# S5 mixer with FFN on one core: modulation products, lag buffers and the order behind the scan

## The chip, the core and the metric

The kernel runs on one core of a Trainium2 chip. A core has five engines that run their own instruction streams: PE (TensorE, matrix products), DVE (VectorE), ACT (ScalarE), POOL (GpSimd) and SP (SyncE), which here only issues DMAs. DMAs are also issued from ACT and POOL. The metric is device time in microseconds (us), the median over runs. A profiled execution gives the trace from which everything below is read.

## The reference

One layer of a diffusion backbone: 1024 latent tokens and 256 context tokens of width 1024. The layer's mixer is a bidirectional S5 state-space model with 64 groups of 16 channels and 64 complex states for each group; a SwiGLU feed-forward follows. Only the latent stream is returned. Everything is float32.

```python
m_l = jnp.split(sc @ ada_w[i] + ada_b[i], N_MOD, axis=-1)       # sc = silu(c), six vectors of 1024
h_l = modulate(rms_norm(x, norm_mix[i]), m_l[0][:, None], m_l[1][:, None])
...
lam_bar = jnp.exp(lam * jnp.exp(log_step.astype(F32))[:, None])
b_bar = ((lam_bar - 1.0) / lam)[..., None] * lax.complex(b_re.astype(F32), b_im.astype(F32))
...
bu = jnp.einsum('lgh,gnh->lgn', u.astype(F32), b_bar)
_, h = lax.associative_scan(_linear_combine, (a, bu), axis=0)
return jnp.einsum('lgn,ghn->lgh', h, c_mat).real, h[-1]
...
g = jax.nn.gelu(y)
return g * jax.nn.sigmoid(g @ w_glu + b_glu)
...
x = x + m_l[2][:, None] * y_l
h_l = modulate(rms_norm(x, norm_ffn[i]), m_l[3][:, None], m_l[4][:, None])
x = x + m_l[5][:, None] * swiglu(h_l, ffn_w1[i], ffn_w3[i], ffn_w2[i])
```

## The kernel before

The order of every engine is the order in which the program is written (a manual schedule); waits come from the data and from the buffers.

The 1280 tokens are cut into chunks of 8 tokens: 32 context chunks and 128 latent chunks. The kernel computes, for each chunk, the state that its 8 tokens add ("sums"); scans these chunk states over the chunks; and then forms the output of a chunk from two parts: the state before the chunk times output weights, and the chunk's own 8 tokens times a table of the products at all 15 lags from -7 to 7 ("lags"). Indices: `hb = 2b + d` is a head, eight groups (b) and a direction (d); `q` is a quarter, 16 groups; a unit `u` has four groups, and `k` is a pair of units.

**Sums** (L558 to L593). For each of the 16 heads PE multiplies the chunks by input weights (L473), ACT copies the result into the states `ST` (L477 to L480), and DVE or POOL adds neighbouring states (`pair`, `ctx_low`). Input weights come from products on DVE or POOL (`bl_make`), an accumulating DMA of POOL (`bl_sum`, L333) and transposes on PE (`bl_tr`, L346). The loop also loads tiles of the modulation weights (`ada_load`, L417) and multiplies them (`ada`, L424): one tile is 128 x 512, and one product is one matrix product of a tile with silu(c). There are 64 such tiles. The first 16 products are done before the sums. `ada_load(m)` issues loads up to tile m; `ada(n)` does the products up to n and keeps eight loads ahead. In the loop, head 9 loads four tiles, head 11 multiplies them and loads four more, and head 14 multiplies these and loads six.

**Scan** (`scan`, L651). DVE alone: 95 dependent steps of four operations (`step`), and in the gaps of the first ones the operations that fill in the states of quarters 0 and 2 (`fill_ops`), two for each step. The fills of quarter 0 are complete after step 36.

**Behind the scan's start**, the string given to `run` (L806) is the order of the other engines' work, while DVE scans. Its letters:

- `An`: modulation products up to n. `M0` to `M2`: their result is copied, transposed and made into columns; M1 ends on ACT, M2 is on POOL.
- `Cqp`: output weights of quarter q, part p (`cl_gen`): two products on POOL, the first into `CL[q]`, the second into a buffer of `cts`, and their sum, which `HOW` puts on PE (L546, two times eight groups, with a copy on ACT, L547) or on an accumulating DMA that POOL issues (`SY`, L549).
- `Ki`: lag products of half a quarter (`k_mats`): for each of two group sets PE's products into `kt`, a copy on ACT into a buffer of `KX`, and a DMA from there to DRAM (`kd`, L633), also issued by ACT.
- `Tu`: the table of unit u, read back from DRAM by a DMA of SP (`toeplitz`, L641, four buffers `KQ`).
- `Rk`: ACT's copies of the states of the first 64 chunks for pair k (L729). `Pk`: PE's inner products of the pair: chunk times table (L747), states times weights (L752). `Yu`: ACT's copy of the result (L803). `Zi`: the same states for the last 64 chunks.
- `Fqh`: POOL's fills of quarters 1 and 3. `Li`, `Gi`: load and sign of `Cs`, from which C is made. `Bi`: ACT's copies of input weights that later K steps read.

Behind the string come the products of the last 64 chunks (`late_mm`, L827), GELU and GLU, and the feed-forward, which fills PE.

Each DMA of SP and ACT takes the next of eight semaphores in the order of the program and waits until the previous DMA on the same one has landed.

Of the kernel before, what the change touches and what calls it, by code (L numbers as in the profile page):

```python
# [17 lines left out]
P = 128  # L18
# [5 lines left out]
T = 8  # L24
G = 64
HC = 16
# [11 lines left out]
def s5_ffn_kernel(tc, a, out):  # L38
    nc = tc.nc
    V, S, E, PE, SY = nc.vector, nc.scalar, nc.gpsimd, nc.tensor, nc.sync  # L40
    ctx = ExitStack()
    with ctx:
# [5 lines left out]
        def view(reg, kb, shape, parts=P):  # L48
            off = int(round(kb * 256))
            n = int(np.prod(shape))  # L50
            v = reg[:parts, off:off + n]
            if len(shape) > 1:
                names = "abcdef"[:len(shape)]
                v = v.rearrange(f"p ({' '.join(names)}) -> p {' '.join(names)}",
                                **{k: d for k, d in zip(names, shape)})
            return v

        R0 = region("r0", 7)
        RA = region("ra", 80.5)
        RU = region("ru", 40)  # L60
        RC = [region(f"c{i}", 16) for i in range(4)]
        RXa, RXc = region("rxa", 8), region("rxc", 8)
# [22 lines left out]
        def small(shape, parts=P):  # L85
            v = view(R0, pos[0], shape, parts)
            pos[0] += int(np.prod(shape)) / 256
            assert pos[0] <= 7, pos[0]
            return v

        cpk = small([HC + 3 * P + HC + 4 + T + 16 + 16])
# [7 lines left out]
        S5 = int(round(pos[0] * 256))  # L99
        cols = small([2, 2, G])  # L100
        LS = small([2, 3, G])
        KD = small([4, 4, HC])
        scs, sc3 = small([8, 2]), small([8, 3])
        rsb, mod2, epsc = small([P + 32]), small([2, T]), small([2])
        mcol = small([4, T])
        ssq, ss2, rt, rtt = small([T, 4]), small([T]), small([T]), small([T])
        frs = small([T])
# [171 lines left out]
        LH = view(RXc, 0, [2, 3, G])  # L279
        SQ = [LS[:, 0], view(RXc, 2, [3, G]), LH[:, 0], LH[:, 1], LS[:, 1]]  # L280

# [122 lines left out]
        NA = 16  # L404
        stg = [view(RA, i, [512]) for i in (20, 22, 0, 2, 4, 6, 8, 10, 40, 42, 44, 46, 12, 14, 16, 18)] + [view(RC[2], 8 * (1 - i // 4) + 2 * (i % 4), [512]) for i in range(8)]
        ada_at = [0, 0]

        def ada_tile(i):

            return stg[i if i < NA else NA + (i - NA) % 4 if i < NA + 8 else NA + (i - NA) % 8]  # L410

        def ada_load(m):
            while ada_at[0] < min(64, m):
                i = ada_at[0]
                h, k, b = i // 32, i // 4 % 8, i % 4
                c0 = (2 + b) * D + 512 * h
                SY.dma_start(ada_tile(i), adaw[k * P:(k + 1) * P, c0:c0 + 512])  # L417
                ada_at[0] += 1

        def ada(n, top=64):  # L420
            for i in range(ada_at[1], n):
                ada_load(min(i + 8, top))
                h, k, b = i // 32, i // 4 % 8, i % 4
                PE.matmul(pm[32 * b:32 * b + 2], sc3[:, k, 1 - h:3 - h], ada_tile(i), start=i < 4, stop=i >= 60,  # L424
                          tile_position=(0, 32 * b))
                ada_at[1] += 1
# [129 lines left out]
        ct0 = [view(RC[1], i, [8, T, HC]) for i in (12, 4)]  # L556
        ct1 = [view(RC[3], i, [8, T, HC]) for i in (0, 4)]
        for hb in range(16):  # L558
            sums(hb)
            if hb == 0:  # L560
                bl_make(6)
                bl_sum(5)
            if hb % 2:
                for i in range(hb + 2, min(hb + 4, 16)):
                    bl_tr(i)
            bl_sum(hb + 6)
            if hb == 1:
                SY.dma_start(BXY[:, 1], a["bxy"][:, 3])
            bl_make(hb + 7)
            if hb < 6:  # L570
                u_ctx(hb + 2)
                u_lat(hb + 2)
                rs_lat(hb + 5)
            if hb >= 1:
                pair(hb - 1, E if hb - 1 in PPAIR else V)
            if hb == 9:
                cs_load(0)
            if hb == 12:
                cs_sign(0)
            if hb == 9:  # L580
                ada_load(NA + 4)
            if hb == 11:
                ada(NA + 4, NA + 4)
                ada_load(NA + 8)
            if hb == 14:
                ada(NA + 8, NA + 8)
                ada_load(NA + 14)
            if hb == 15:
                ada_load(NA + 16)
            if hb in CLOW:  # L590
                ctx_low(*CLOW[hb])
            for part in CGEN.get(hb, ()):
                cl_gen(0, part, ct0[part % 2], E if part == 3 else SY)  # L593
# [10 lines left out]
        kt = pA.tile([P, 2, 240], F32, tag="r3", name="kt")  # L604
        S.copy(kt.rearrange("p a b -> p (a b)"), cpk[:, 0:1].to_broadcast([P, 480]))


        KX = [cpk[:, HC + P:HC + P + 15 * HC], cols.rearrange("p a b g -> p (a b g)")[:, 0:15 * HC]]
        BBc = PW.rearrange("p t i (d e) -> p (t i) d e", d=2)
        KQ = [view(RA, 2 * i, [4, P]) for i in range(4)]  # L610
        HSe = [(RA, 8 + 4 * i) for i in range(2)]
        KD_ = [dr.tile([P, 4, 15 * HC], F32, tag=f"kd{q}", name=f"kd{q}") for q in range(4)]
# [4 lines left out]
        def k_mats(q, hq):  # L617

            for g_ in range(2):
                gq = 2 * hq + g_  # L620
                quarters = [(gi * 4 + gq, kt[32 * gi:32 * gi + HC, g_], (0, 32 * gi)) for gi in range(4)]
                for gl, kv, tp in quarters:
                    PE.matmul(kv[:, 128:240], bb(q, 1, gl), CL[q][:, 1, gl, 7:0:-1], start=True, stop=True, tile_position=tp)
                for gl, kv, tp in quarters:
                    PE.matmul(kv[:, 0:112], bb(q, 0, gl), CL[q][:, 0, gl, 6::-1], start=True, stop=True, tile_position=tp)
                for gl, kv, tp in quarters:
                    l0 = tp[1]
                    PE.matmul(kv[:, 112:128], ident[:, l0:l0 + HC], KD[:, q, gq], start=True, stop=False, tile_position=tp)
                for d in range(2):
                    for gl, kv, tp in quarters:  # L630
                        PE.matmul(kv[:, 112:128], bb(q, d, gl), Cs[q % 2][:, 0, d, gl], start=False, stop=d == 1, tile_position=tp)
                S.copy(KX[g_], kt[:, g_])
                S.dma_start(KD_[q][:, gq], KX[g_])  # L633

        def toeplitz(u):

# [117 lines left out]

        scan()
        inner, hse = {}, {}
        ct2 = [view(RC[3], i, [8, T, HC]) for i in (8, 12)]
        ct3 = [view(RXc, 4, [8, T, HC]), view(RU, 16, [8, T, HC])]
        cts = [ct0 * 2, ct1 * 2, ct1 * 2, ct2 + ct3]

        HSl = [hstate(RXc, 0), hstate(RXc, 4), hstate(RA, 8), hstate(RA, 0)]
        order = (6, 7, 4, 5, 0, 1, 2, 3)
# [6 lines left out]
        def run(prog):  # L769


            for w in prog.split():
                op, i = w[0], int(w[1:])
                if op == "A":
                    ada(i)
                elif op == "M":
                    mod_cols(i)
                elif op == "K":
                    k_mats(*divmod(i, 2))
                elif op == "Z":  # L780
                    late_restack(i)
                elif op == "L":
                    cs_load(i, S)
                elif op == "G":
                    cs_sign(i)
                elif op == "B":
                    j = 48 - HC * i
                    S.copy(BBc[:, :, :, j:j + HC], BB[:, :, HC * i:HC * i + HC].rearrange("p d g h -> p g d h"))
                elif op == "C":
                    q, part = divmod(i, 10)  # L790
                    cl_gen(q, part, cts[q][part], HOW[q][part])
                elif op == "F":
                    fill(*divmod(i, 10), *((RA, 12) if i < 20 else (RXc, 4)))
                elif op == "T":
                    toeplitz(i)
                elif op == "R":
                    hse[i] = hstate(*HSe[len(hse) % 2])
                    for d in range(2):
                        restack(hse[i], 4 * i, d, 0, 64, (S, S, S, S))
                elif op == "P":  # L800
                    inner_mm(i, hse[i])
                elif op == "Y":
                    S.copy(yview(i), inner[i])  # L803

        HOW = ((PE,) * 4,) + ((SY,) * 4,) * 2 + ((SY, SY, SY, PE),)
        run("A36 C00 A40 C01 A44 C02 A48 C03 A52 A56 K0 A60 K1 A64 L2 C10 T0 T1 T2 T3 C11 M0 M1 C12 C13 F10 F11 G2 B3 B2 K2 K3 L3"  # L806
            " R0 P0 C20 T4 T5 R1 P1 Y0 Y1 C21 M2 T6 T7 G3 C22 C23 R2 Y2 Y3 P2 R3 Y4 Y5 P3 Y6 Y7 K4 K5 T8 T9 T10 T11"
            " C30 C31 C32 R4 P4 R5 C33 K6 K7 Y8 Y9 P5 Y10 Y11 T12 T13 T14 T15 F30 F31 R6 P6 R7 Y12 Y13 P7 Z1 Z0 Y14 Y15")
        psA.__exit__(None, None, None)


# [289 lines left out]
        G2 = region("c1", 16, R32)  # L1101
# [307 lines left out]
```

## Time and profile before

| | us |
|---|---|
| median of 3 runs | 1119.66 (1116.76 to 1124.03) |
| profiled execution, its own time | 1125.31 |
| profiled execution, its span | 1123.5 |
| PE busy | 997.6 |
| DVE busy | 821.6 |
| POOL busy | 646.7 |
| ACT busy | 414.9 |

The span goes from the first to the last instruction. A row of a timeline reads: start, duration, engine, line, operation, what it writes and reads, how many instructions were merged, and in brackets the idle time before it and what ended that. "128x512 f32" are partitions and elements. SPq and ACTq are DMA issues of SP and ACT. A float32 matrix product counts as two passes, so that x8 at L424 is four products. An `r` in a name is the tile `R0`, `c` one of the four tiles `RC`, `ra`, `ru`, `rxa` and `rxc` the other regions. Some names of releasers are of an engine that had long been done: the wait of R0 at 206.35 is put down to DVE, while ACT was issuing a load.

### The profile page before, as it was taken

What the parts mean: (1) busy time and instruction counts of PE and PEld (TensorE: products, weight loads), DVE (VectorE), ACT (ScalarE), POOL (GpSimd) and SP (SyncE); (2) the same over time, 40 slices, a digit from 0 to 9 for tenths busy, and PEclk for the clock granted to TensorE, in tenths of its full rate; (3) what the DMA queues carried; (4) which work ended last, traced back from release to release, by engine and by line L of the source; (5) the groups of instructions that cost most, each with busy time, mean ns of one, the idle gap of its engine ahead of it and who ended that gap; (6) DMA issues with size and microseconds to landing.
All of it is one profiled execution on the core that took longest, in us unless ns stands there. A gap on an engine that the chain in (4) does not pass through costs nothing. (4 is left out here: it accounts for less than half of the span.)

```text
span 1123.5 us, 16549 instructions
## 1 busy us (share of the span) xinstructions
PE 997.6 (89%) x6088; PEld 802.1 (71%) x6088; DVE 821.6 (73%) x1689; ACT 414.9 (37%) x871; POOL 646.7 (58%) x503
## 2 busy tenths in 40 slices
PE   4689795647979999879999999999999999999997
PEld 1268422535869997667888888888888888888875
DVE  8989699980777796998666766666666666666657
ACT  4279512634834455222222222222222222222236
POOL 4389678882373343865555555555555555555563
PEclk9699897768999999899999999999999999999999
DMA  9966679753411201101111111111111111111104
GB/s 351 339 139 122 166 255 238 162 113 73 159 50 65 76 1 57 56 20 57 57 57 43 37 36 54 57 57 57 57 57 57 57 57 57 57 57 57 49 27 150
DMA packets 51457, 103.64 MB, mean 92 GB/s; under 512 B 4272, under 2 KB 25008, under 8 KB 49328
## 3 DMA queue, kind: packets, MB, share of 16 engines
q1 hardware_dynamic: 43456, 85.67, 23.0%
q0 software_dynamic: 3600, 13.11, 6.3%
q10 hardware_dynamic: 4320, 3.81, 1.0%
q8 instruction: 48, 0.79, 0.3%
q14 instruction: 33, 0.27, 0.1%
HBM read 83.30 MB, written 6.16 MB: 80 GB/s over the span
## 5 line engine op out<-in xcount | busy, mean ns | idle before, releaser
L70 POOL TENSOR_TENSOR c<-rxc,c 128x512 fp32r<-128x512 f32 x128 | 169.3, 1337 | 186.9 <-ACT c L1063 182.9
L70 DVE TENSOR_TENSOR ru<-pd,ru 128x512 f32<-128x512 f32 x336 | 227.0, 691 | 2.4 <-PE pd L1119 2.3
L1119 PE MATMUL pu<-ra,c 128*128 128x512 f32 x432 | 168.5, 390 | 1.3 <-POOL c L70 1.2
L1118 PE MATMUL pu<-ra,c 128*128 128x512 f32 x432 | 168.2, 389 | 0.6 <-DVE ra L70 0.6
L1117 PE MATMUL pu<-ra,c 128*128 128x512 f32 x432 | 168.4, 390 | 0.3 <-ACT ra L1063 0.3
L1063 ACT CAST c<-rxc 128x512 fp32r<-128x512 f32 x128 | 76.7, 616 | 186.2 <-POOL rxc L70 107.2
L1117 PE MATMUL pd<-c 128*128 128x512 f32 x336 | 133.2, 397 | 10.9 <-DVE ru L70 10.9
L1118 PE MATMUL pd<-c 128*128 128x512 f32 x336 | 132.4, 394 | 0.0
L1119 PE MATMUL pd<-c 128*128 128x512 f32 x336 | 132.2, 393 | 0.0
L70 DVE TENSOR_TENSOR ru<-pu,ru 128x512 f32<-128x512 f32 x84 | 57.9, 690 | 87.5 <-PE pu L1119 53.3
L70 POOL TENSOR_TENSOR c<-ru,c 128x1024 fp32r<-128x1024 f32 x22 | 53.2, 2420 | 85.8 <-ACT c L861 77.1
L1119 PEld LDWEIGHTS pu<-ra,c 128*128 128x128 f32 x432 | 81.1, 188 | 19.7 <-POOL c L70 3.0
L1118 PEld LDWEIGHTS pu<-ra,c 128*128 128x128 f32 x432 | 81.1, 188 | 17.7 <-POOL c L70 0.9
L1117 PEld LDWEIGHTS pu<-ra,c 128*128 128x128 f32 x432 | 81.1, 188 | 17.6 <-ACT ra L1063 0.8
L1117 PEld LDWEIGHTS pd<-c 128*128 128x128 f32 x336 | 64.1, 191 | 26.2 <-DVE ru L70 12.9
L1119 PE MATMUL pu<-c,c 128*128 128x512 f32 x192 | 74.8, 390 | 0.3 <-POOL c L70 0.3
L1117 PE MATMUL pu<-c,c 128*128 128x512 f32 x192 | 74.9, 390 | 0.0
L1118 PE MATMUL pu<-c,c 128*128 128x512 f32 x192 | 74.7, 389 | 0.0
L1119 PEld LDWEIGHTS pd<-c 128*128 128x128 f32 x336 | 64.1, 191 | 13.6
L1118 PEld LDWEIGHTS pd<-c 128*128 128x128 f32 x336 | 64.2, 191 | 13.2
L70 POOL TENSOR_TENSOR c<-rxc,rxa 128x1024 f32<-128x1024 f32 x30 | 62.1, 2130 | 12.1 <-PE pw L546 7.4
L70 DVE TENSOR_TENSOR ru<-ru,rxa 128x512 f32<-128x512 f32 (+1 forms) x62 | 62.2, 1003 | 7.1 <-ACT ru L1262 3.1
(292 smaller groups left out, 2219.7 us busy)
## 6 DMA issues: line engine op xcount, KB each, us to landing
c<-in_ada_w SPq DMA_DIRECT2D x48, 256.0 KB, 4.8
ru<-in_w SPq DMA_DIRECT2D x22, 512.0 KB, 3.6
c<-c POOLq DMA_DIRECT2D x20, 512.0 KB, 5.5
rxc<-in_w SPq DMA_DIRECT2D x38, 256.0 KB, 4.3
rxc<-in_w SPq DMA_DIRECT2D x19, 512.0 KB, 5.0
ra<-in_ada_w SPq DMA_DIRECT2D x8, 1024.0 KB, 9.9
ru<-in_xT SPq DMA_DIRECT2D x4, 1024.0 KB, 6.3
ra<-in_ada_w SPq DMA_DIRECT2D x16, 256.0 KB, 6.0
```

What stands on the lines that cost most here:

```text
L70: eng.tensor_tensor(out=o, in0=x, in1=y, op=op)
L1063: S.copy(o[0], x)
L1117: PE.matmul(pu, wh, bh, start=start, stop=False)
L1118: PE.matmul(pu, wh, bl, start=False, stop=False)
L1119: PE.matmul(pu, wl, bh, start=False, stop=stop)
```

## The change

1. The products at heads 11 and 14 leave the loop of the sums. The loop only loads eight tiles (head 10, 13 and 14) into eight buffers in place of four; the first products behind the 16 of the start are now A24 to A32, behind the scan's start. All 64 are still done.
2. `KX` gets a third buffer, in R0 where the last scan powers and the row scales `rsb` (moved for that) are no longer needed, and the K steps take the three in turn.
3. In the string, K0, K1 and T0 to T3 come ahead of A52 to A64, and R0 and P0 ahead of M0 and M1; K2 and K3 come behind P0, M2 ahead of C20, C22 and C23 behind Y7, Y8 and Y9 ahead of C33, and R5 behind K7.
4. Quarter 3's second products get other buffers: part 0 the place RU 16 (which P3 reads, and Y8 and Y9 write), part 1 as before, parts 2 and 3 both RXc 4. Part 2's sum moves from the accumulating DMA to PE.

```diff
@@ -99,9 +99,10 @@
         LS = small([2, 3, G])
+        rsb = small([P + 32])
         KD = small([4, 4, HC])
         scs, sc3 = small([8, 2]), small([8, 3])
-        rsb, mod2, epsc = small([P + 32]), small([2, T]), small([2])
+        mod2, epsc = small([2, T]), small([2])
@@ -406,8 +407,7 @@
         def ada_tile(i):
-
-            return stg[i if i < NA else NA + (i - NA) % 4 if i < NA + 8 else NA + (i - NA) % 8]
+            return stg[i if i < NA else NA + (i - NA) % 8]
@@ -577,16 +577,10 @@
-            if hb == 9:
+            if hb == 10:
                 ada_load(NA + 4)
-            if hb == 11:
-                ada(NA + 4, NA + 4)
-                ada_load(NA + 8)
-            if hb == 14:
-                ada(NA + 8, NA + 8)
-                ada_load(NA + 14)
-            if hb == 15:
-                ada_load(NA + 16)
+            if hb in (13, 14):
+                ada_load(NA + 6 if hb == 13 else NA + 8)
@@ -605,7 +599,9 @@
-        KX = [cpk[:, HC + P:HC + P + 15 * HC], cols.rearrange("p a b g -> p (a b g)")[:, 0:15 * HC]]
+        kx0 = S5 + 4 * G + 3 * G
+        KX = [cpk[:, HC + P:HC + P + 15 * HC], cols.rearrange("p a b g -> p (a b g)")[:, 0:15 * HC], R0[:, kx0:kx0 + 15 * HC]]
+        kxn = [0]
@@ -629,8 +625,10 @@
-                S.copy(KX[g_], kt[:, g_])
-                S.dma_start(KD_[q][:, gq], KX[g_])
+                kx = KX[kxn[0] % 3]
+                kxn[0] += 1
+                S.copy(kx, kt[:, g_])
+                S.dma_start(KD_[q][:, gq], kx)
@@ -754,9 +752,8 @@
-        ct2 = [view(RC[3], i, [8, T, HC]) for i in (8, 12)]
-        ct3 = [view(RXc, 4, [8, T, HC]), view(RU, 16, [8, T, HC])]
-        cts = [ct0 * 2, ct1 * 2, ct1 * 2, ct2 + ct3]
+        ct3 = [view(r, kb, [8, T, HC]) for r, kb in ((RU, 16), (RC[3], 12), (RXc, 4))]
+        cts = [ct0 * 2, ct1 * 2, ct1 * 2, ct3 + ct3[2:]]
@@ -802,10 +799,10 @@
-        HOW = ((PE,) * 4,) + ((SY,) * 4,) * 2 + ((SY, SY, SY, PE),)
-        run("A36 C00 A40 C01 A44 C02 A48 C03 A52 A56 K0 A60 K1 A64 L2 C10 T0 T1 T2 T3 C11 M0 M1 C12 C13 F10 F11 G2 B3 B2 K2 K3 L3"
-            " R0 P0 C20 T4 T5 R1 P1 Y0 Y1 C21 M2 T6 T7 G3 C22 C23 R2 Y2 Y3 P2 R3 Y4 Y5 P3 Y6 Y7 K4 K5 T8 T9 T10 T11"
-            " C30 C31 C32 R4 P4 R5 C33 K6 K7 Y8 Y9 P5 Y10 Y11 T12 T13 T14 T15 F30 F31 R6 P6 R7 Y12 Y13 P7 Z1 Z0 Y14 Y15")
+        HOW = ((PE,) * 4,) + ((SY,) * 4,) * 2 + ((SY, SY, PE, PE),)
+        run("A24 A28 A32 C00 A36 C01 A40 A44 C02 A48 C03 K0 K1 L2 T0 T1 T2 T3 A52 A56 C10 C11 C12 C13 A60 A64 F10 F11 R0 P0 M0 M1 Y0 Y1"
+            " G2 K2 K3 L3 R1 P1 T4 T5 T6 T7 Y2 Y3 B3 B2 M2 C20 C21 G3 R2 P2 R3 Y4 Y5 P3 Y6 Y7 C22 C23 K4 K5 T8 T9 T10 T11"
+            " C30 C31 C32 R4 P4 Y8 Y9 C33 K6 K7 R5 P5 Y10 Y11 T12 T13 T14 T15 F30 F31 R6 P6 R7 Y12 Y13 P7 Z1 Z0 Y14 Y15")
```

How this moves the instructions is shown at three places, each engine's order before and then now. The new kernel's line numbers differ by a few (L347 is L346 of before, L639 is L641). The first place is PE from the transposes of heads 13 and 14 to the first output weights; L473 are sums, L424 products.

```order
L346 MATMUL pw<-r_60,c_63 128x128 x16
L424 MATMUL pm<-c_65,r_60 2x512 x4
L473 MATMUL pw<-ru,c_66 64x160 x16
L473 MATMUL pw<-ru,c_65 64x160 x16
L346 MATMUL pw<-r_60,c_64 128x128 x8
L473 MATMUL pw<-ru,c_65 64x160 x16
L424 MATMUL pm<-c_65,r_60 2x512 x4
L473 MATMUL pw<-ru,c_66 64x160 x16
L424 MATMUL pm<-c_65,r_60 2x512 x12
L546 MATMUL pw<-c_63,r_60 128x512
```

Now:

```order
L347 MATMUL pw<-r_60,c_63 128x128 x16
L473 MATMUL pw<-ru,c_66 64x160 x16
L473 MATMUL pw<-ru,c_65 64x160 x16
L347 MATMUL pw<-r_60,c_64 128x128 x8
L473 MATMUL pw<-ru,c_65 64x160 x16
L473 MATMUL pw<-ru,c_66 64x160 x16
L424 MATMUL pm<-c_65,r_60 2x512 x16
L546 MATMUL pw<-c_63,r_60 128x512
```

Two sets of four products have left the sums, and sixteen in place of twelve stand between the sums and C00. The second place is SP from the load of Cs 0 to the tables of quarter 2; in_ada_w are the tile loads, kd the tables.

```order
L526 DMA rxc<-in_cxy 128x4x256
L417 DMA c_65<-in_ada_w 128x512 x48
L641 DMA ra<-kd_1297 128x4x128 x4
L641 DMA ra<-kd_1298 128x4x128 x4
L641 DMA ra<-kd_1299 128x4x128 x4
```

Now:

```order
L526 DMA rxc<-in_cxy 128x4x256
L417 DMA c_65<-in_ada_w 128x512 x39
L639 DMA ra<-kd_1281 128x4x128 x4
L417 DMA c_65<-in_ada_w 128x512 x9
L639 DMA ra<-kd_1282 128x4x128 x4
L639 DMA ra<-kd_1283 128x4x128 x4
```

The first four tables have moved ahead of the last nine tile loads. The third place is POOL behind the fills of quarter 1 (the rows that read ra): the 128x1024 rows are output weights of quarter 2, and the rows of r_60 are M2.

```order
L70 TENSOR_TENSOR ra<-ra 128x16x2x8 x2
L70 TENSOR_TENSOR c_65<-rxc,rxa 128x1024
L70 TENSOR_TENSOR c_66<-rxc,rxa 128x1024
L549 DMA c_65<-c_66 128x1024
L70 TENSOR_TENSOR c_65<-rxc,rxa 128x1024
L70 TENSOR_TENSOR c_66<-rxc,rxa 128x1024
L549 DMA c_65<-c_66 128x1024
L70 TENSOR_TENSOR r_60<-r_60 128x32
L698 COPY r_60<-r_60 128x8
L70 TENSOR_TENSOR r_60<-r_60 128x8 x2
L70 TENSOR_TENSOR c_65<-rxc,rxa 128x1024
```

Now:

```order
L70 TENSOR_TENSOR ra<-ra 128x16x2x8 x2
L70 TENSOR_TENSOR r_60<-r_60 128x32
L696 COPY r_60<-r_60 128x8
L70 TENSOR_TENSOR r_60<-r_60 128x8 x2
L70 TENSOR_TENSOR c_65<-rxc,rxa 128x1024
L70 TENSOR_TENSOR c_66<-rxc,rxa 128x1024
L549 DMA c_65<-c_66 128x1024
L70 TENSOR_TENSOR c_65<-rxc,rxa 128x1024
```

M2 has moved from behind C21 to ahead of C20; C22 and C23 still follow C21.

## The prediction

> **What bounds the kernel now.** I read the stages first, then the engines' timelines from 105 to 285 us, because the change touches nothing else. In the busy time by stage a row has the stretch, its length, the busy time of PE, PEld, DVE, ACT and POOL, the clock granted to TensorE, and DMA.
>
> ```profile
> span 1123.5 us, 16549 instructions
> 139.40:285.00 145.60, 97.19 (x1148) 60.82 (x1150) 112.67 (x542) 54.76 (x124) 102.98 (x91) 0.81 0.66 166
> 285.00:1123.50 838.50, 800.95 (x4116) 676.88 (x4112) 591.39 (x883) 279.64 (x540) 453.47 (x320) 0.99 0.17 58
> ```
>
> From 285 us on PE is busy for 801 of 838 us: that part only shifts. Between 139 and 285 no engine is full, so a chain of waits sets the time there. The timelines of PE and DVE show where it begins:
>
> ```profile
> 117.68 1.06 PE L346 MATMUL pw<-r,c 128*128 128x128 f32 x8 [1.44 <-DMA c<-c]
> 120.11 1.79 PE L424 MATMUL pm<-c,r 128*2 128x512 f32 x2 [1.36 <-DMA c<-in_ada_w]
> 126.75 4.15 PE L473 MATMUL pw<-ru,c 128*64 128x160 f32 x56
> 136.34 2.39 PE L473 MATMUL pw<-ru,c 128*64 128x160 f32 x32
> 135.98 0.43 DVE L70 TENSOR_TENSOR ltb<-ra,lta 128x256 f32<-128x256 f32 x1 [9.28 <-ACT ra L477]
> 150.68 0.29 DVE L70 TENSOR_TENSOR ltb<-ra,lta 128x128 f32<-128x128 f32 x1
> 250.25 0.29 DVE L70 TENSOR_TENSOR ra<-ltc,ra 128x128 f32<-128x128 f32 x1
> ```
>
> PE ends a transpose at 118.74, stands before four modulation products whose tiles are still in flight, and goes on with the sums at 126.75. DVE has finished at 126.70 (135.98 less 9.28) and waits for those sums. Then the scan's 95 steps run without a gap from 150.68 to 250.54, 1.051 us each. After it the lags, their tables and POOL decide:
>
> ```profile
> 141.61 6.44 PE L424 MATMUL pm<-c,r 128*2 128x512 f32 x16 [0.56 <-DMA c<-in_ada_w]
> c<-in_ada_w SPq DMA_DIRECT2D x48, 256.0 KB, 4.8
> 161.19 1.04 PE L424 MATMUL pm<-c,r 128*2 128x512 f32 x8
> 166.76 3.70 PE L546 MATMUL pw<-c,r 128*128 128x512 f32 x8
> 175.32 0.56 PE L623 MATMUL kt<-c,c 128*16 128x112 f32 x4
> 189.34 1.12 PE L693 MATMUL pw<-r,c 128*128 128x128 f32 x4 [1.73 <-ACT c L689]
> 190.49 0.26 ACT L695 COPY r<-pw 128x16 f32<-128x16 f32 x2 [1.21 <-PE pw L693]
> 191.03 4.13 SPq L641 DMA_DIRECT2D ra<-kd  x4
> 198.50 3.99 POOL L70 TENSOR_TENSOR c<-rxc,rxa 128x1024 f32<-128x1024 f32 x2
> 204.05 3.78 PE L747 MATMUL pw<-ra,ru 128*128 128x128 f32 x16
> 206.35 7.00 ACT L729 COPY ra<-ra 64x256 f32<-64x256 f32 x16 [1.73 <-DVE lta L70]
> 208.29 7.48 SPq L641 DMA_DIRECT2D ra<-kd  x4
> 208.59 0.54 POOL L70 TENSOR_TENSOR r<-r 128x32 f32<-128x32 f32 x1
> 219.30 0.88 POOL L549 DMA_DIRECT2D c<-c  x1 [0.30 <-POOL c L70]
> c<-c POOLq DMA_DIRECT2D x4, 512.0 KB, 6.7
> 227.86 2.04 PE L747 MATMUL pw<-ra,ru 128*128 128x128 f32 x8 [3.94 <-DMA ra<-kd]
> 229.84 3.42 PE L752 MATMUL pw<-c,ra 128*64 128x128 f32 x32
> 233.19 0.39 PE L623 MATMUL kt<-c,rxa 128*16 128x112 f32 x8
> ```
>
> K0 starts at 175.32, T0 is issued at 191.03, R0 and R1 run together only at 206.35 (on ACT behind K2 and K3), P3 waits for T7 until 227.86, K4 starts at 233.19. The rest repeats one pattern:
>
> ```profile
> 234.43 0.33 ACTq L633 DMA_DIRECT2D kd<-r  x1
> 235.29 0.36 ACT L632 COPY r<-kt 128x240 f32<-128x240 f32 x1 [0.90 <-PE kt L631]
> 238.48 0.36 ACT L632 COPY r<-kt 128x240 f32<-128x240 f32 x1 [2.83 <-DMA kd<-r]
> 240.12 0.33 ACTq L633 DMA_DIRECT2D kd<-r  x1
> 242.45 6.52 SPq L641 DMA_DIRECT2D ra<-kd  x4
> 247.53 1.40 POOL L70 TENSOR_TENSOR rxc<-ra,r 128x256 f32<-128x256 f32 x2 [0.55 <-DMA c<-rxc]
> 249.51 4.03 PE L747 MATMUL pw<-ra,ru 128*128 128x128 f32 x16 [9.91 <-DMA ra<-kd]
> 257.42 1.52 POOL L70 TENSOR_TENSOR ra<-ra,rxc 128x256 f32<-128x256 f32 x2
> 269.21 4.65 SPq L641 DMA_DIRECT2D ra<-kd  x4
> 274.39 1.13 PE L747 MATMUL pw<-ra,ru 128*128 128x128 f32 x8 [2.05 <-DMA ra<-kd]
> 276.69 1.55 PE L747 MATMUL pw<-ra,ru 128*128 128x128 f32 x8 [1.17 <-DMA ra<-kd]
> 281.26 2.05 PE L747 MATMUL pw<-ra,ru 128*128 128x128 f32 x16
> ```
>
> A third lag copy waits 2.83 us for the first buffer's write; the first table T8 is ready 7.06 us after its issue, T12 5.18 us, and T13 2.30 us after T12.
>
> **Step 1, products out of the sums.** PE takes up the sums behind the transpose at 118.9 instead of 126.75. DVE covers nothing there: it is done at 126.70, and the sums that it waits for now end at 135.98 - 7.9 = 128.1. The other four products (1.04 us) stood behind those sums. The scan runs from 142.8 to 242.7. Gain 7.9; bounds 6.5 (if the last transposes wait 1.4 for their accumulating write) and 9.3 (DVE's whole wait).
>
> **Step 2, products behind the scan's start.** The sums end on PE at 138.73 - 7.9 - 1.0 = 129.8. Of the sixteen products A24 to A32 eight have their tiles; the other eight tiles are issued as those products free buffers, 130 to 132. If the last lands 4.8 after its issue, that is 136.8; if the first takes 4.8 and seven follow at 0.8 (6.44 us for eight at 141.61), it is 140.5. I take 139.2, nearer to the second, since the load of Cs 1 shares the engines. Four C steps of 3.70 and sixteen products of 0.26 make 19.0: 158.2, and behind ACT's last copy K0 at 159.3, 16.0 earlier. The eight moved products cost nothing beyond this as PE waits for tiles there anyway. C0's products on POOL take 3.99 a pair, less than PE's 3.70 and 1.04, and move up with the sums. With tiles at 1.0 us K0 slips by 5.
>
> **Step 3, three lag buffers.** The third copy no longer waits, only the fourth, until the first write has landed (234.43 to 238.48: 4.05). A lag pair takes 1.25 less (0.36 + 0.90, one copy's cycle): 5.7 instead of 6.93 from K4's start to its last write at 240.12. K1's last write leaves at 165.0, T0 is issued 2.3 later (as 240.12 to 242.45) at 167.3, and T3 lands 5.18 + 3 x 2.30 = 12.1 behind it: 179.4.
>
> **Step 4, first in line on SP.** T0 to T3 stand ahead of the last nine tile loads. Five of these also wait for the tables and a lag write to land, since eight DMA semaphores go round. The last tile is issued at about 180 and lands near 184.5, and A60 and A64 stand ahead of P0 on PE. R0 needs the scan's step 36, 142.8 + 37.8 = 180.6, and half of 7.00 for its eight copies: 184.1. The two meet. PE has idled and runs P0 as slowly as at 204.05: 3.78, and about 2.7 for the second half (at most 3.42; 1.9 if it speeds up as 3.78 does to 2.05): 191.0.
>
> The Trainium skill, TensorE: Matmul & The Clock Gate, Part 1, says that the array falls to half its clock after an idle window of about 3.4 us and needs as long a busy one to come back. The rows agree: 3.78 at 204.05 against 2.05 at 281.26 for the same sixteen. Without that rule P0 and the sum would be 2.5 us better; with it the sum is the one here.
>
> **Step 5, second products (C2).** POOL now has M2 ahead of C20; M2 waits for M1, and so for P0. M1's transposes and copies take 1.7 (189.34 to 191.0), M2, four small operations from 208.59, 1.2: C20 starts at 193.9 instead of 198.50. C22 and C23 stand later in the program but at the same place on POOL: nothing. With M2 no longer between, C23's write is issued at 219.30 - 4.6 - 1.2 = 213.5 and lands 6.7 later, 220.2. P3 arrives with it: K2 starts behind M1 at 193, its pair's 5.7 and 2.3 put T4's issue at 201, and T7 is ready 12.1 later (as T15 after T12) at best, 19.6 (208.29 to 227.86) at worst: 213 to 220.6. I take 217.4, as T6 and T7 no longer wait for P1 but still share with C21 to C23; 4.0 for P3's rest gives 221.4. So K4 starts at 221.4 instead of 233.19: 11.8 gained.
>
> **Step 6, the end.** K5's and K7's last writes gain 1.25 each. C30's second product now writes where P3 reads: POOL waits until about 220, then C30, C31 (3.99 + 0.30 + 0.88) and C32 follow, and PE adds C32 from 233 to 237, ahead of T9 at 238: covered. C33 is added by PE after P4, as before. F30 now waits for that addition (247) and F31 ends 11.4 later (247.53 to 258.94); R6 follows at about 259, beside R5 and the tables: even, or up to 1 us lost. Sum: 11.8 + 2.5 - 0.3 = 14.0. The span goes from 1123.5 to 1109.5. The profiled run took 1125.31, 5.65 above the median 1119.66; from the median, **1105.7 us**.
>
> **Rivals.**
> *The wait moves to the tile loads.* For it: T0 to T3 run beside the accumulating writes of C11 to C13, as T7 did beside C22's and C23's. T3 then lands 4.6 later at 184, A64 ends at 189, and P0, C20 and P3 move with it: gain 9.4, 1110.3. Against: at T12 and T13 four tables landed at 2.3 us each with little beside them, and C11's write comes only when PE has read C03. The Trainium skill, DMA: Bandwidth & Descriptors, Issuing engines are not separate DMA queues, says that DMAs of all issuers run on the same 16 engines and interleave. By that rule this rival is the case; T7's row agrees.
> *Nothing binds at SP.* The tables land as T13 did or sooner, P0 runs fast, P3 isn't held by T7: C20 starts at 189, 4.9 earlier still: gain 18.9, 1100.8.
> *Slower.* K0 comes late because the tiles taken out of the sums queue behind it: as T0 stays ahead of nine loads, each us at K0 is one at A64 and P0. The gain of 14 is gone when K0 starts at 173.3; at 178 it is 1124.4, and over 1% slower from 184.5. Against: eight tiles would then cost 14 us more, and the trace shows 0.8 each.
> *The change doesn't do what it says* holds for C22 and C23 alone, priced at nothing above.
>
> **Chances.** Forecast 0.50, tile loads 0.25, nothing binds 0.18, slower 0.07. The likeliest is 1105.7, by itself 1102 to 1109 (1.4 each way from steps 1 and 2, 2.5 from P0's clock). The range reaches from 1098 (nothing binds, and 3 us better) to 1114 (tile loads, and 4 us worse). A measurement tells about 1% from no change: 1108.5 to 1130.9. Faster by over 1%: 0.92 of the forecast, all of nothing binds, 0.04 from tile loads: 0.68; slower 0.05; within 0.27.
>
> **What would show it.** Right: the scan starts at 143 and DVE's wait of 9.28 is under 2; K0 near 159, T0 near 167; third lag copies without a wait; A64 and R0 within 3 us of each other near 184; K4 at 221; the late products (L827 before) from 271. Wrong: C00 on PE after 144 (step 2), A64 after 189 (step 4), C20 on POOL after 198 (step 5), P6 and P7 waiting for R6 and not for the tables (step 6). The sum falls altogether if the scan isn't earlier, or if PE's 801 us behind it change.

## The result and the profile after

The changed kernel takes 1128.7 us (median of 6 runs, 1127.43 to 1130.41) and the kernel before 1119.75 beside it (6 runs, 1116.76 to 1124.03). The ratio is 1.0081, with a 95% interval of 1.0059 to 1.0103: some 9 us slower, where 14 us faster were predicted.

The first fence has the stages of the changed kernel's profiled execution (1129.6 us, span 1127.8), with the columns of the stages shown before.

```profile
139.40:285.00 145.60, 96.28 (x1089) 56.68 (x1090) 103.84 (x521) 51.73 (x117) 92.91 (x80) 0.80 0.61 152
285.00:1127.80 842.80, 805.65 (x4176) 681.28 (x4172) 593.08 (x889) 283.51 (x549) 455.93 (x324) 0.99 0.17 58
```

The second stage has taken 60 of PE's products over from the first (4176 against 4116), because the late products begin later, at 289.61 instead of 285.04. From them to the end the kernel takes 838.2 us, against 838.5 before. So the loss lies ahead of 290 us. PE's timeline shows where:

```profile
119.19 4.02 PE L473 MATMUL pw<-ru,c 128*64 128x160 f32 x56
143.62 3.70 PE L546 MATMUL pw<-c,r 128*128 128x512 f32 x8
147.25 2.90 PE L424 MATMUL pm<-c,r 128*2 128x512 f32 x8
153.71 3.01 PE L424 MATMUL pm<-c,r 128*2 128x512 f32 x16
166.26 0.38 PE L619 MATMUL kt<-c,c 128*16 128x112 f32 x6
171.32 1.94 PE L424 MATMUL pm<-c,r 128*2 128x512 f32 x14
195.28 6.47 PE L424 MATMUL pm<-c,r 128*2 128x512 f32 x18 [22.02 <-DMA c<-in_ada_w]
201.68 2.05 PE L745 MATMUL pw<-ra,ru 128*128 128x128 f32 x16
206.15 0.39 PE L619 MATMUL kt<-c,c 128*16 128x112 f32 x8
225.65 2.08 PE L745 MATMUL pw<-ra,ru 128*128 128x128 f32 x8 [5.91 <-DMA ra<-kd]
239.32 0.39 PE L619 MATMUL kt<-c,rxa 128*16 128x112 f32 x8
289.61 3.66 PE L824 MATMUL pe<-c,rxc 128*64 128x128 f32 x64
```

The sums stand at 119.19, as they should, and K0 at 166.26 is 9 us earlier than before. Then PE does seven products and stands for 22.02 us before the ninth-last tile. A64 ends at 201.7, P0 follows at once, K2 comes behind P0 and M1, and K4 is 6 us later than before. The other engines' rows say what PE waits for and who waits for PE:

```profile
129.61 0.43 DVE L70 TENSOR_TENSOR ltb<-ra,lta 128x256 f32<-128x256 f32 x1 [2.06 <-ACT ra L477]
172.37 0.33 ACTq L631 DMA_DIRECT2D kd<-r  x1
176.17 6.81 SPq L639 DMA_DIRECT2D ra<-kd  x4
183.03 14.47 SPq L417 DMA_DIRECT2D c<-in_ada_w  x9
DMA to landing us min/median/max: 9.0/9.0/9.1
181.35 1.68 ACT L727 COPY ra<-ra 64x256 f32<-64x256 f32 x4 [0.43 <-DVE ra L70]
206.60 0.24 POOL L70 TENSOR_TENSOR r<-r 128x32 f32<-128x32 f32 x1 [13.24 <-ACT r L693]
208.31 4.00 POOL L70 TENSOR_TENSOR c<-rxc,rxa 128x1024 f32<-128x1024 f32 x2 [0.77 <-ACT rxc L529]
218.53 6.82 SPq L639 DMA_DIRECT2D ra<-kd  x4
```

DVE's wait of 9.28 has become 2.06. SP issues the four tables at 176.17, 3.8 us behind K1's last lag write, and only then, from 183.03 to 197.5, the last nine tile loads. The fifth row is the time from issue to landing, 9.0 us where the median was 4.8 before; it covers two of these loads. By the trace's semaphore events, T3 landed at 194.0 and the nine loads from 195.2 to 200.7, 3.5 to 12.2 us behind their issue. The last load waited for its buffer until the ninth-last tile's product had read it, and so was issued only at 197.18. The DMA engines were not idle meanwhile; in the stretch of PE's wait their share (the second figure from the end) is 0.92:

```profile
173.30:195.20 21.90, 0.00 (x0) 0.00 (x0) 21.90 (x126) 3.26 (x8) 19.16 (x22) 0.56 0.92 198
```

R0's copies are done at 183.0, so P0 waits for nothing but A64. POOL is idle for 13.24 us before M2, and C20 starts at 208.31 instead of 198.50.

### The profile page after: what moved, and what is told of

Same layout as the page of the kernel before. It is cut to its first block, busy times and chain, and to the rows that moved or that the text cites. A ratio compares the mean times of both kernels' runs of the same rounds, so it can differ in the third digit from the quotient of the medians.

```text
span 1127.8 us, 16572 instructions
## 1 busy us (share of the span) xinstructions
PE 1003.2 (89%) x6096; PEld 804.0 (71%) x6096; DVE 819.8 (73%) x1689; ACT 415.9 (37%) x873; POOL 648.8 (58%) x502
## 5 line engine op out<-in xcount | busy, mean ns | idle before, releaser
L1114 PE MATMUL pu<-ra,c 128*128 128x512 f32 x432 | 168.4, 390 | 0.3 <-ACT ra L1060 0.3
L1114 PEld LDWEIGHTS pd<-c 128*128 128x128 f32 x336 | 64.1, 191 | 26.2 <-DVE ru L70 12.9
```

Of the source, the lines that this page charges most:

```text
L1114: PE.matmul(pu, wh, bh, start=start, stop=False)
```

## The experiments

The string is cut to the part that moves. An execution's start varies by up to 5 us before the sums begin, so the table's times are set to the kernel before: from each is taken what the run's DVE stood behind the kernel before at one operation of the sums (101.35 us there; the column "off"). Ratios are those of timed runs to runs of the kernel before on the same chip, with 95% intervals; a point of the ratio is 1%, some 11 us. The times of a row come from one execution; the times in the text and in the fences are as that execution's trace has them.

| kernel | ratio | off | K0 | A64 ends | P0 | K2 | T4 issued | K4 | late products |
|---|---|---|---|---|---|---|---|---|---|
| before | | 0.0 | 175.3 | 187.6 | 204.0 | 190.4 | 208.3 | 233.2 | 285.0 |
| before, again | 1.0009 (0.9984 to 1.0035) | 0.6 | 172.3 | 183.8 | 198.2 | 186.1 | 200.7 | 223.9 | 275.1 |
| changed | 1.0081 (1.0059 to 1.0103) | 0.9 | 165.4 | 200.9 | 200.8 | 205.3 | 217.7 | 238.5 | 288.8 |
| e1 loads first | 1.0003 (0.9973 to 1.0033) | 3.8 | 165.7 | 192.1 | 192.1 | 196.5 | 205.1 | 228.7 | 278.7 |
| e2 tables on ACT | 1.0060 (1.0034 to 1.0086) | 4.4 | 164.9 | 196.7 | 196.6 | 203.2 | 215.8 | 236.0 | 284.7 |
| e3 M2 back | 1.0057 (1.0028 to 1.0085) | 0.7 | 169.0 | 204.7 | 204.6 | 209.1 | 221.5 | 241.8 | 290.1 |
| e4 part 1 alone | 0.9984 (0.9954 to 1.0015) | 5.0 | 169.7 | 184.1 | 198.3 | 187.5 | 200.8 | 223.8 | 275.3 |
| e5 part 1, buffers | 0.9924 (0.9900 to 0.9948) | 3.5 | 168.7 | 180.4 | 194.8 | 183.8 | 198.2 | 218.4 | 270.8 |
| e8 K2 K3 early | 1.0037 (1.0010 to 1.0064) | -0.2 | 168.4 | 206.5 | 206.4 | 196.7 | 207.6 | 232.3 | 290.5 |
| e9 and G2, M2 | 1.0038 (1.0004 to 1.0072) | 0.0 | 168.9 | 206.1 | 206.0 | 197.6 | 207.4 | 231.4 | 287.1 |
| e10 and A, M0 | 0.9876 (0.9827 to 0.9925) | 0.6 | 167.2 | 178.4 | 192.5 | 180.7 | 195.0 | 217.6 | 266.1 |
| f1 A alone | 0.9981 (0.9964 to 0.9998) | 3.5 | 169.7 | 181.4 | 190.0 | 197.0 | 209.8 | 230.3 | 278.6 |
| f2 e10, K2 late | 0.9953 (0.9920 to 0.9985) | 1.3 | 172.4 | 187.6 | 193.3 | 199.8 | 208.2 | 229.7 | 278.7 |
| f3 e10, old C3 | 0.9888 (0.9859 to 0.9918) | 1.7 | 169.5 | 181.1 | 195.3 | 184.5 | 198.1 | 220.2 | 272.3 |
| g1 e1, no accum. | 0.9935 (0.9898 to 0.9972) | 4.6 | 166.5 | 184.6 | 184.6 | 189.7 | 199.0 | 218.1 | 275.7 |
| g2 no accum. | 1.0020 (1.0004 to 1.0036) | 3.5 | 168.3 | 195.6 | 195.5 | 200.0 | 208.4 | 232.1 | 280.2 |

The theory at the start: the nine tile loads lie behind the four tables, and everything else is late because of that. The rivals: it is POOL's order (M2 ahead of C20); the gain of the early sums is spent elsewhere; or the DMA engines are full, whoever is first.

**e1, the loads first.**

```diff
- K0 K1 L2 T0 T1 T2 T3 A52 A56 C10 C11 C12 C13 A60 A64 F10 F11 R0
+ K0 K1 A52 A56 A60 A64 L2 T0 T1 T2 T3 C10 C11 C12 C13 F10 F11 R0
```

> The changed kernel, with the products A52 to A64 and so the last nine tile loads ahead of T0 to T3 on SP. Theory (the nine tile loads lie behind the four tables, on SP and on the DMA engines): the loads are issued from about 172 us on, A64 ends at 180 to 185 instead of 201.7, T0 is issued at 178 to 181 and P0 starts at 188 to 192, held by R0 and T1; 9 to 13 us less than the changed kernel, 1116 to 1120. Rival (the accumulating writes of C11 to C13 fill the DMA engines, whoever stands first): A64 ends early, but T0 and T1 land as much later, P0 starts after 198 and the time is within 4 us of the changed kernel. Rival (POOL's order alone is what costs): no change.

1120.3 us, some 9 less than the changed kernel (0.78 points of the ratio). The size is the theory's, the places are not: A64 ends at 196 instead of 180 to 185, T0 is issued at 183.5 instead of 178 to 181, and P0 starts at 195.9 instead of 188 to 192. PE's products, the tables on SP, and the time of the loads to landing:

```profile
180.73 1.86 PE L424 MATMUL pm<-c,r 128*2 128x512 f32 x2 [4.20 <-DMA c<-in_ada_w]
183.46 10.23 SPq L639 DMA_DIRECT2D ra<-kd  x4
DMA to landing us min/median/max: 10.1/11.0/12.0
```

The last row covers three of the eight loads issued from 175.6 on, the last ones; by the semaphore events all eight took 5.1 to 12.0 us, with a median of 7.7. They had no table ahead of them on SP. So the order on SP is only a part of it.

**e2, the tables from ACT.** T0 to T3 are issued by ACT; nothing else moves.

```diff
-            SY.dma_start(KQ[u % 4], src)
+            (S if u < 4 else SY).dma_start(KQ[u % 4], src)
```

> The changed kernel, with T0 to T3 issued by ACT instead of SP; all else keeps its place. Theory, in the form that the issuing queue is what holds the loads: SP issues the nine loads from about 172 on, they land beside the tables, A64 ends by 186 and P0 starts at 190 to 193 (ACT issues the tables until about 183 and copies R0 until 190): 8 to 11 us less than the changed kernel. Rival (the engines that carry the tables hold the loads, whichever queue they come from): the loads still land after T3, A64 ends at 195 or later, and the time is within 4 us of the changed kernel.

1127.7 us, within 2 us of the changed kernel, and A64 at 201.1: these are the rival's figures. Its mechanism is not what the trace shows. What SP waited for from 160 to 200 us (total, times, longest), and the last tile's products on PE:

```profile
SPq L417 <- DMA ra<-kd: 8.8, 1, 8.8
199.23 1.87 PE L424 MATMUL pm<-c,r 128*2 128x512 f32 x2 [6.33 <-DMA c<-in_ada_w]
```

Eight of the nine loads now go out early, from 168.0 to 184.2, and have all landed by 191.8, while T3 lands only at 199.5 (semaphore events). But the ninth takes a DMA semaphore that T0 has, and SP waits 8.8 us until that table has landed; PE is done with the eighth at 192.9 and stands 6.33 us for the ninth. So e2 doesn't tell what the other queue is worth. With a semaphore of its own for the ninth load, P0 could have started some 6 us earlier at most, when T1 has landed (194.8 instead of 201.03); this is an estimate from those two times, and was not run. The Trainium skill, DMA: Bandwidth & Descriptors, Issuing engines are not separate DMA queues, says that another issuer saves only the time of issuing, since all DMAs run on the same 16 engines. The trace agrees that they interleave: the loads that SP issued from 178 to 184.2, beside C12's and C13's writes and ACT's tables, took 7.6 to 8.8 us, against 4.8 before. The equal times of the two kernels don't show it.

**e3, M2 back behind C21.**

```diff
- B3 B2 M2 C20 C21 G3
+ B3 B2 C20 C21 M2 G3
```

> The changed kernel, with M2 behind C21 on POOL as in the kernel before. POOL is free at 193.4 and no longer waits for M1: C20 starts at about 193.5 instead of 208.3. Theory (P0's delay reaches the end through K2 and the tables T4 to T7, not through POOL): P0 stays at 201.7, T4 is issued at about 218, P3 still waits for T7, and the time falls by 0 to 4 us. Rival (C20 behind M2 carries the loss): C23 is done some 14 us earlier, K4 starts by 228, and the time falls by 9 to 13 us.

1127.3 us: M2's place alone is not what costs. But C20 did not start at 193.5 either, so the run doesn't tell what an early C20 is worth. POOL's row:

```profile
211.91 4.01 POOL L70 TENSOR_TENSOR c<-rxc,rxa 128x1024 f32<-128x1024 f32 x2 [15.16 <-ACT rxc L529]
```

It waits for the sign G2 on ACT, which the change has put behind Y0 and Y1, and so behind P0. In the kernel before, G2 stood ahead of K2.

**e4, the first part alone**: the kernel before, with the products out of the sums and eight tile buffers, the string beginning `A24 A28 A32 C00 A36 C01 A40 A44 C02 A48 C03 A52 A56 K0 A60 K1 A64`, and the rest as before. **e5** adds the third lag buffer.

> The kernel before, with the products taken out of the sums (eight tile buffers, and A24 to A32 ahead of C00, in the order of the changed kernel as far as C03); lags, tables, M2 and the last C products as before. Theory (steps 1 and 2 are a gain by themselves): the scan ends at 243, K0 starts at 166 to 170 and the late products start 5 to 8 us earlier: 1112 to 1115. Rival (the sixteen products behind the scan's start cost what the sums gain, since the tiles come at 0.8 us or slower): K0 starts at 173 or later, within 3 us of the kernel before.

> As the run with part 1 alone, and three lag buffers instead of two. There K1's first copy waited 5.57 us and K3's 2.18 for the lag writes of two buffers ago. Theory (step 3 is a gain): K1's third copy no longer waits, T0 is issued 4 to 7 us earlier, K3 ends 2 us earlier, K5 and K7 1.25 each: 2 to 5 us less than part 1 alone, 1114 to 1117. Rival (the lags are not on the path there; P0 stands behind K3 and R0 anyway and the tables share the DMA engines): within 2 us of part 1 alone.

e4 can't be told from no change (1119.4 us, where the theory had 1112 to 1115); e5 is 0.76% faster (1112.8) and 0.60 points below e4, somewhat more than expected. ACT's third and fourth copies of K1, in e4 the first two rows, in e5 the others:

```profile
185.81 0.36 ACT L630 COPY r<-kt 128x240 f32<-128x240 f32 x1 [7.84 <-DMA kd<-r]
188.74 0.36 ACT L630 COPY r<-kt 128x240 f32<-128x240 f32 x1 [2.58 <-DMA kd<-r]
```

```profile
178.84 0.36 ACT L630 COPY r<-kt 128x240 f32<-128x240 f32 x1 [3.37 <-PE kt L627]
183.07 0.36 ACT L630 COPY r<-kt 128x240 f32<-128x240 f32 x1 [3.88 <-DMA kd<-r]
```

In e4 K0 comes earlier, and the third copy then waits 7.84 us for the first lag write, which was on its way beside the tile loads (the 5.57 and 2.18 in my expectation are PE's waits for such copies). The third buffer takes that wait away (the third copy now waits for PE alone); the fourth copy still waits 3.88. The early sums gave something only together with the buffer. The buffer without the early sums was not run, so how the gain of e5 divides between the two stays open.

**e8 and e9**, K2 and K3 ahead of P0 in the changed kernel; e9 with G2 ahead of them and M2 behind C21 as well. The edit shown is e9's.

```diff
- C13 A60 A64 F10 F11 R0 P0 M0 M1 Y0 Y1 G2 K2 K3 L3 R1 ... B2 M2 C20 C21 G3
+ C13 F10 F11 R0 G2 K2 K3 L3 A60 A64 P0 M0 M1 Y0 Y1 R1 ... B2 C20 C21 M2 G3
```

> The changed kernel, with K2 K3 L3 between R0 and A60 instead of behind P0, M1 and Y1. Theory (two chains end together at K4, tables T4 to T7 behind K2 and K3, and C20 behind P0, M1 and the sign G2; either alone gives little): T4 is issued at 205 to 210 instead of 218.5, P2 and P3 no longer wait for tables, but C20 still starts at about 208 and K4 at 235 to 238: 1 to 4 us less than the changed kernel. Rival (only the tables bind): K4 starts by 230, 9 us or more less. Rival (K2 waits for the writes of C12 and C13 and keeps A60, A64 and P0 up): P0 after 203, no change or slower.

> As the run before it, with G2 ahead of K2 too and M2 behind C21, so that POOL's C20 waits neither for P0 nor for M1 (M2 alone gave nothing: C20 then waited for G2, which stood behind Y0 and Y1 on ACT). Theory (both chains): C20 starts at 194 to 197 instead of 208.3, C23 is written by 217, T4 is issued at 205 to 210, K4 starts at 226 to 230: 9 to 13 us less than the changed kernel, 1116 to 1120. Rival (tables and accumulating writes share the DMA engines, and what is drawn ahead comes back as longer transfers): K4 at 234 or later, within 5 us of the changed kernel.

e8 takes 1125.8, 0.44 points below the changed kernel, with intervals that overlap (its profiled execution, 1131.7, was the slowest of its ten). T4 is at 207.4 and the time 2.9 us less by the medians, as the theory had it; but K4 comes at 232.1, ahead of the theory's 235 to 238, and P0 only at 206.2, as the second rival had it. e9 takes 1126.2, no less than e8, and misses the theory's 1116 to 1120 widely. Its rows on PE and POOL:

```profile
197.55 1.02 PE L424 MATMUL pm<-c,r 128*2 128x512 f32 x1 [21.66 <-DMA c<-in_ada_w]
210.74 4.00 POOL L70 TENSOR_TENSOR c<-rxc,rxa 128x1024 f32<-128x1024 f32 x2 [14.74 <-PE pw L691]
```

K2 comes no earlier than 197.6, since the last product of A56 still stands ahead of it and waits 21.66 us for its tile. And C20 waits for M1 (L691) with neither M2 nor G2 ahead of it: it writes `CL[2]`, which lies in RC[2], where the last tiles' buffers and M0's copy `r8` lie until PE has read them. A64 ends at 206.1 there though its tiles are in place, since K2 and K3 now stand ahead of A60: the last eight products take 2.0 us, from 204.18. So K2 hangs on the late tiles by PE's order, and C20 by its buffer. This led to e10 and f1.

**f1 and e10.** f1 puts only the products A52 to A64 back to where they stood before: A52 and A56 ahead of K0, A60 ahead of K1 and A64 behind it, and so ahead of most DMAs of C1. The edit shown is f1's. e10 does that in e9, with M0 and M1 behind C13, ahead of K2, and P0 behind L3.

```diff
- C03 K0 K1 L2 T0 T1 T2 T3 A52 A56 C10 C11 C12 C13 A60 A64 F10
+ C03 A52 A56 K0 A60 K1 A64 L2 T0 T1 T2 T3 C10 C11 C12 C13 F10
```

> The changed kernel, with nothing but the products A52 to A64 put back to where they stood before (A52 A56 K0 A60 K1 A64, then L2 and T0 to T3). Theory (the whole loss is that A60 and A64 come late, since C20 and K2 both stand behind P0 and M1, and these behind A64): A64 ends at 178 to 182 instead of 201.7, P0 starts at 190 to 195, held by the tables T0 and T1, K4 at 226 to 231: 8 to 13 us less than the changed kernel, 1115 to 1120. What is then left against e10 (1107) is P0, M1 and Y0 standing ahead of K2 and C20. Rival (the whole gain of e10 is A64's): 1105 to 1110.

> As e9, and the products A52 to A64 placed as in the kernel before (A52 A56 K0 A60 K1 A64), M0 M1 behind C13: the sums, three buffers, T0 to T3 ahead of C10 and the new C3 stay. Theory: A64 ends 12 us behind K0, as before, at 183 to 187; P0 starts at 192 to 198 and K4 at 220 to 226; 12 to 18 us less than the changed kernel, 1111 to 1117. Rival (steps 5 and 6 of the change have a loss of their own, in T8 to T15 and the last C products): K4 as early, but the late products start less than 5 us earlier than in the changed kernel: 1122 or more.

f1 takes 1119.9 us, 1.00 points of the ratio below the changed kernel (11 us); e10 takes 1107.0, 1.24% faster than the kernel before and less than the 1111 to 1117 expected; it has the lowest median of all, from four runs. f1's P0, K2 and C20:

```profile
193.47 3.79 PE L745 MATMUL pw<-ra,ru 128*128 128x128 f32 x16 [8.60 <-DMA ra<-kd]
200.52 0.39 PE L619 MATMUL kt<-c,c 128*16 128x112 f32 x8
202.67 4.01 POOL L70 TENSOR_TENSOR c<-rxc,rxa 128x1024 f32<-128x1024 f32 x2 [0.78 <-ACT rxc L529]
```

A64 ends at 184.9 there, and P0 stands 8.60 us before the tables; K2 and C20, behind P0 and M1, wait with it. In e10 they don't. Its last tile product, C20, K4, the late products and the first stage:

```profile
177.96 1.02 PE L424 MATMUL pm<-c,r 128*2 128x512 f32 x2 [1.84 <-DMA c<-in_ada_w]
192.29 3.99 POOL L70 TENSOR_TENSOR c<-rxc,rxa 128x1024 f32<-128x1024 f32 x2
218.16 0.39 PE L619 MATMUL kt<-c,rxa 128*16 128x112 f32 x8
266.63 1.59 PE L824 MATMUL pe<-c,rxc 128*64 128x128 f32 x26
139.40:266.60 127.20, 96.00 (x1145) 58.57 (x1144) 105.78 (x524) 55.81 (x125) 94.72 (x84) 0.88 0.66 172
```

C20 starts without a wait, and as much of PE's work as before fits into 127.2 us instead of 145.6.

**f2 and f3** take one piece out of e10 each: f2 puts K2, K3 and L3 behind Y1 again, f3 has the last C products (buffers, C32, order) as before the change.

> As e10, but K2 K3 L3 behind Y1 as in the changed kernel. Theory (C20 and the tables are two chains to K4): C20 stays at 192 to 195, K2 moves from 187 to 196 to 199, T4 from 195.5 to 207 to 210, P3 waits for T7 and K4 starts at 222 to 227 instead of 218: 4 to 8 us more than e10, 1111 to 1115. Rival (only POOL's chain from C20 to C23 sets K4): within 2 us of e10.

> As e10, with the last C products as before: C32 by an accumulating write, C30's second product in the old place, and C33 K6 K7 ahead of Y8 Y9. Theory (step 6 gains: from K4 to the late products e10 takes 48.4 us, the run with part 1 and three buffers, with the old C3, 52.5): 2 to 5 us more than e10, 1109 to 1112. Rival (the prediction's: even, within 1 us).

f2: 1114.8 us, 0.77 points more than e10, as the theory of two chains had it, though the two intervals touch (0.9920 and 0.9925). K4 at 231.0 lies above its 222 to 227 and C20 at 199.6 above its 192 to 195, in part because that execution was late from K0 on. f3: 1108.8 us. Its interval overlaps e10's, so the runs don't tell "even" from the 2 to 5 us that I expected; in the traces K4 to the late products takes 52.1 against 48.5.

**The kernel before, again.**

> The kernel before, once more, for a second profiled execution. The first took 1125.3 us, above most runs of that kernel. If the stretch from the sums to the late products varies from run to run by itself, K4 starts 3 to 8 us earlier here, counted from the sums; if only the stretch before the sums varies, K4 stands 130 us behind the second group of sums (103.0 to 233.2), as there.

Its timed runs agree with the other runs of that kernel. The profiled execution does not agree with the first one: K4 stands 121.2 us behind the second group of sums, 9.0 less than there, where 3 to 8 were expected. Its first stage and its late products:

```profile
139.40:275.70 136.30, 92.06 (x1145) 57.63 (x1147) 110.82 (x537) 54.51 (x123) 101.18 (x88) 0.85 0.67 175
275.69 1.48 PE L827 MATMUL pe<-c,rxc 128*64 128x128 f32 x24
```

The same program took 9.3 us less from 139.4 to the late products. A single execution of this stretch is no base for a few microseconds.

**g1 and g2**, e1 and the changed kernel with the sums of C10 to C13 done by POOL's additions instead of accumulating writes. In e1 the DMA queues took, from 176 to 194 us (packets, MB, share of the 16 engines' time; q0 are POOL's writes, q1 is SP):

```profile
q0 software_dynamic: 400, 1.44, 44.5%
q1 hardware_dynamic: 1921, 2.49, 42.2%
```

```diff
-        HOW = ((PE,) * 4,) + ((SY,) * 4,) * 2 + ((SY, SY, PE, PE),)
+        HOW = ((PE,) * 4,) + ((E,) * 4, (SY,) * 4) + ((SY, SY, PE, PE),)
```

> As e1 (the nine tile loads ahead of T0 to T3), and the sums of C10 to C13 done by additions on POOL (2.0 us each) instead of accumulating writes. Theory (the writes hold the loads; in e1 they took 44.5% of the 16 DMA engines' time from 176 to 194 us): the eight loads behind K1 land 5 to 7 us after their issue instead of 11.0, and A64 ends at 181 to 186 instead of 196. Rival (the engines are held by the tables, the lag writes and the load of Cs): 9 us or more, and A64 at 193 or later.

> The changed kernel (T0 to T3 ahead of the nine loads), and the sums of C10 to C13 on POOL instead of accumulating writes. Theory (the writes share the engines with the tables): T0 to T3 land within 10 to 14 us of T0's issue instead of 17.3, the loads behind them in 5 to 8 instead of 9.0, and A64 ends at 190 to 196 instead of 201.7. Rival (the tables alone take the time, in pieces of 512 bytes): 16 us or more, and A64 at 199 or later.

The loads' time from issue to landing, in g1 (for the same last three loads as in e1) and then in g2 (for the same two as in the changed kernel):

```profile
DMA to landing us min/median/max: 4.1/6.3/6.4
DMA to landing us min/median/max: 6.8/6.8/6.9
```

6.3 instead of 11.0, and 6.8 instead of 9.0; by the semaphore events the median of all eight loads is 5.7 instead of 7.7, and that of all nine 6.9 instead of 9.0. In g2 T3 lands 11.8 us behind T0's issue (179.93 to 191.7, from the same events) instead of 17.8 (176.17 to 194.0; the 17.3 of my expectation ended at the first part of that table to land). A64 ends 7.5 and 5.3 us earlier by the table. Its own times, 189.2 and 199.1, lie 3 us above what I wrote in both; K0 was 2 and 6 us later in these executions than in those that the figures came from. The times are 1111.9 and 1121.3 us, 0.68 and 0.61 points below e1 and the changed kernel. So the accumulating writes do hold the loads and the tables up.

## Why the prediction was wrong

**Step 1 was right.** The scan ended 8 us earlier by the common clock, and DVE's wait went to 2.06. By itself it gave nothing clear of the spread (e4, 0.9954 to 1.0015): the lag copies took it back.

**Step 2 was 7 us short at K0** (159.3 predicted, 166.26). C00 came at 143.62 and not at 139.2: 4.4. And the sixteen products behind it took 8.1 (the stretches between the C steps: 147.25 to 150.07, 153.71 to 156.64, 160.28 to 162.63) where I had 4.2: PE caught up with the loads and took the last products of each group as their tiles landed (semaphore events). I had priced them with tiles in place. (K0 began without the 1.1 that I had put behind C03.)

**Step 3 was right**: the third copy waits for nothing, and from K0 to K1's last write it took 6.1 (5.7). T0 then came 3.8 behind it and not 2.3.

**Step 4 failed**, at "The last tile is issued at about 180 and lands near 184.5". The last tile was issued at 197.18 and landed at 200.7; A64 ended at 201.7, 17.2 late. The terms: K0 7.0; K0 to T0 1.9 (9.9 for 8.0); T0's issue to T3's landing 5.7 (17.8 for 12.1); the last product behind that landing 2.6 (7.7 for 5.1), for the last load also waits for the buffer of the ninth-last tile, which itself landed only at 195.2. g2 shows the third to be the accumulating writes: without them it is 11.8. I had used T12 and T13, landings with little beside them, and set aside T7's row, which showed the other case. f1 shows what the whole step costs: with A52 to A64 where they stood, 11 us of the time come back.

**Step 5 followed its chain.** By the prediction's own terms P0's end moves by 14.6 (17.2, less 2.6 since P0 ran at 2.05 + 1.97 directly behind the products and not at the slow 3.78); C20 moved by 14.4 (193.9 to 208.31), K4 by 17.9 (221.4 to 239.32; the 3.3 more is mostly T4, issued 12.9 behind P0's end and not 10), the late products by 18.6 (271 to 289.61). That K2, and C20 through M2, stood behind P0 was in the prediction. What I did not see is that C20 hangs on P0 by two more ties, G2 and RC[2], so that moving M2 alone frees nothing (e3). f1 has A64 at the time that I forecast (184.9 for 184.5), and still P0 waits for tables and K4 comes at 233.8. e10, with these freed, comes near what I wrote for the change: C20 at 192.3 (193.9), K4 at 218.2 (221.4), the late products at 266.6 (271), 1.24% gained (14.0 of 1119.66 is 1.25%). That the two gains are equal is in part luck: e10 is another order, with the nine loads ahead of the tables again and P0 at 193.1 instead of 184.5. P0's two speeds are in the rows above: 2.05 behind 6.47 us of products in the changed kernel, 3.79 behind 8.60 idle in f1. The clock granted in these two stretches, the third figure from the end, was 1.00 and 0.50:

```profile
201.68:205.60 3.92, 3.92 (x50) 3.63 (x49) 3.92 (x24) 0.58 (x1) 0.00 (x0) 1.00 0.00 0
193.47:197.26 3.79, 3.79 (x18) 3.56 (x20) 3.79 (x22) 0.00 (x0) 3.63 (x6) 0.50 0.50 142
```

The Trainium skill, TensorE: Matmul & The Clock Gate, Part 1, has half the clock after an idle window; the rows agree.

**Step 6** was about right: from K4 to the late products 50.3 against 51.9 before, 1.6 less for 2.2 predicted. f3 leaves its worth open within the runs' spread.

**The rivals.** "The wait moves to the tile loads" had the right mechanism: T3 4.6 later beside C11 to C13 (5.7 measured). But it added that to an A64 of 184.5 and stopped at 189. "Slower" came true without its condition: K0 came at 166.3, well ahead of its 173.3. By its working, each us at A64 is one of the time, the gain of 14 is gone with A64 at 198.5. That was passed by 3.2, which alone makes 1122.9.

**The rest of the miss** is the base. By the two profiled executions the late products start 4.6 us later; by the medians the loss is 9.0. The execution from which I took the waits stood 5.6 above its median, the changed kernel's 0.9. I read waits such as K4's 233.19 as the kernel's, and "before, again" has 223.9.

## What to carry to other kernels

Before a transfer is put first in a queue, follow what is put behind it to everything that waits for it, by data and by buffers as well as by order; here the last modulation tile held P0, and through it the next lags, a sign and the buffer of the next output weights. Take a transfer's time from a row with the same company on the DMA engines as it will have, and price a product whose operand is still in flight by the landing, not by the product. And profile the base twice: what differs between two executions of one kernel is no gain that a change can claim.

## What the runs showed of the hardware

- Accumulating writes are dear to their neighbours: in e1 1.44 MB of them took 44.5% of the 16 engines' time in 18 us, 2.49 MB of SP's loads and tables 42.2%, so for a byte 1.8 times as much. Without them (g1) the last three of eight 256 KB loads landed in 4.1 to 6.4 us instead of 10.1 to 12.0.
- A DMA semaphore can hold a load more than its queue does: with the tables on ACT's queue eight of nine loads had landed by 191.8, and the ninth, which shares a semaphore with T0, was held for 8.8 us (e2). The loads issued from 178 to 184.2, beside those tables and two accumulating writes, took 7.6 to 8.8 us, against 4.8 before.
- One program's stretch of some 140 us varied by 9.3 us between two executions, with the same order on every engine.
